# Loading and storing an unpooling kernel's images in three contiguous sections, with reads that span several partitions' rows

## The chip, the cores and the metric

One core of one Trainium2 chip. The metric is the time of one execution in device microseconds (us), lower is better. A ratio is the mean time of one kernel's fast runs over the mean of the other's fast runs of the same rounds on the same chip, so it is not quite the ratio of the medians that are quoted beside it.

## The reference

For each element of `x` (16 x 64 images of 32 x 32, float32) an index from 0 to 3 says in which corner of its 2 x 2 block of the output (64 x 64 an image) it goes. The other three get zero.

```python
for i in range(h):
    for j in range(w):
        idx = indices[b, c, i, j]
        output[b, c, i * 2 + idx // 2, j * 2 + idx % 2] = x[b, c, i, j]
```

The indices arrive as 64-bit integers, of which VectorE reads the low words. So 4.19 MB of x and 8.39 MB of indices are read and 16.78 MB are written: 29.36 MB.

## The kernel before

Each of the 128 partitions holds eight consecutive images. x comes in one load, the indices in two (three images of each partition, then five), all issued by SyncE as its first instructions. VectorE makes one output corner at a time, `(index == corner) * x`. After every two images of a partition, a store of 4 MB is issued on the same SyncE queue. In the trace the transfers land in the order of issue on this queue (x at 12.39 us, the indices at 19.67 and 31.80, the first store at 41.52). Cuts are marked.

```python
G = 2                    # images of a partition in one store
FIRST = 3                # images of a partition in the first index load
x_v = x.rearrange("b (ch t) h w -> (b ch) (t h w)", t=T)            # T = 8
idx_v = indices.rearrange("b (ch t) h w -> (b ch) (t h w)", t=T).bitcast(I32)
out_v = out.rearrange("b (ch g t) oh ow -> g (b ch) (t oh ow)", g=NG, t=G)
# ... out_t: three buffers, the fourth store uses the first again
program.first(nc.sync.dma_start(out=x_t, in_=x_v).then_inc(x_in, 16))
for half, part in enumerate((slice(0, cut), slice(cut, None))):     # cut = FIRST * 2 * N
    program.first(nc.sync.dma_start(out=idx_t[:, part], in_=idx_v[:, part])
                  .then_inc(idx_in[half], 16))
# ... VectorE waits for x_in and idx_in[0], at image FIRST for idx_in[1]
            for pidx in range(4):
                op = nc.vector.scalar_tensor_tensor(
                    out=o_c[:, k : k + n, :, pidx // 2, :, pidx % 2],
                    in0=idx_c[:, t : t + n], scalar=pidx, in1=x_c[:, t : t + n],
                    op0=mybir.AluOpType.is_equal, op1=mybir.AluOpType.mult)
            if k + n == G:
                op.then_inc(made, 1)
for g in range(NG):
    nc.sync.wait_ge(made, g + 1)
    nc.sync.dma_start(out=out_v[g], in_=out_t[g]).then_inc(stored if g else stored_0, 16)
```

## Time and profile before

| | before |
|---|---|
| time, median (range) of 6 runs | 71.62 us (71.49 to 71.75) |
| span of the profiled execution | 70.5 us |
| DMA engines at work | 97.4% of the span |
| VectorE at work | 50% of the span |
| loads landed / last store landed | 31.80 / 70.46 us |
| first store issued | 28.73 us |

The page's row of 40 slices of the span (busy share of the 16 DMA engines in tenths, then GB/s; a packet is booked whole in a slice, so single slices swing):

```profile
DMA  9779798899988999969899997979798999979790
GB/s 260 316 316 558 335 558 344 376 432 446 595 372 372 395 511 535 418 298 521 372 428 465 409 483 335 539 316 558 335 521 372 446 446 409 483 335 539 316 558 37
```

The second is the windows around the place where the queue passes from loads to stores, near 31 us (columns: stretch, length, VectorE, GpSimd, clock, DMA share, GB/s):

```profile
4.00:20.00 16.00, 0.19 (x1) 0.00 (x0) 1.00 1.01 434
20.00:28.00 8.00, 8.00 (x4) 0.00 (x0) 1.00 1.06 461
28.00:33.00 5.00, 5.00 (x5) 0.00 (x0) 1.00 0.90 390
33.00:40.00 7.00, 7.00 (x7) 0.00 (x0) 1.00 1.04 449
40.00:69.00 29.00, 15.40 (x7) 0.00 (x0) 1.00 1.01 434
```

The time from issue to landing of the two index loads:

```profile
DMA to landing us min/median/max: 19.2/25.1/30.9
```

The later one, issued near 0.9 us, lands near 31.8. The 390 in the middle window is a matter of booking: the neighbours have 461 and 449.

### The profile page before, as it was taken

Reading aid. Unit: us, or ns where it says so; the run is one execution under the profiler, and the core shown is the slowest. Engines: PE = TensorE matmul, PEld = TensorE weight load, DVE = VectorE, ACT = ScalarE, POOL = GpSimd, SP = SyncE. Lnnn points to the kernel's source line nnn. Section 1 sums busy time; section 2 is a strip of 40 time slices with the busy share of each in tenths; the row PEclk is TensorE's granted clock in tenths of the full one; section 3 lists DMA queues with packets and bytes.
Section 4 is the critical chain, followed back from the end, with each engine's and each line's share of the span. In section 5 each row is a group of like instructions: output and inputs, shape, how many; then the busy total and the mean of one; then the engine's idle time right before and its main releaser. Section 6 shows DMA issues by size and latency. Waiting matters only on the chain.

```text
span 70.5 us, 72 instructions
## 1 busy us (share of the span) xinstructions
DVE 35.6 (50%) x20; POOL 0.2 (0%) x4
## 2 busy tenths in 40 slices
DVE  0000000000079999999999999999999400000000
POOL 1000000000000000000000000000000000000000
DMA  9779798899988999969899997979798999979790
GB/s 260 316 316 558 335 558 344 376 432 446 595 372 372 395 511 535 418 298 521 372 428 465 409 483 335 539 316 558 335 521 372 446 446 409 483 335 539 316 558 37
DMA packets 1008, 29.36 MB, mean 416 GB/s; under 512 B 112, under 2 KB 112, under 8 KB 112
## 3 DMA queue, kind: packets, MB, share of 16 engines
q1 hardware_dynamic: 1008, 29.36, 97.4%
HBM read 12.58 MB, written 16.78 MB: 416 GB/s over the span
## 4 chain that ended last, share of the span: by engine, by line
DVE 46%; DVEq 4%; issue 1%
DVE out_t L130 46%; DVEq L180 4%
## 5 line engine op out<-in xcount | busy, mean ns | idle before, releaser
L130 DVE SCALAR_TENSOR_TENSOR out_t<-idx_t,x_t 128x2048 f32<-128x2048 int32 (+1 forms) x20 | 35.6, 1857 | 19.8 <-DVEq L119 19.8
L166 POOL MEMSET const-uint8-127<- 128x1 uint8 x1 | 0.1, 103 | 0.0
L166 POOL MEMSET const-bfloat16-1.0<- 128x1 bf16 x1 | 0.1, 102 | 0.0
L166 POOL MEMSET const-float32-0.0<- 128x1 f32 x1 | 0.1, 99 | 0.2 <-issue 0.2
L166 POOL MEMSET const-float32-1.0<- 128x1 f32 x1 | 0.1, 99 | 0.0
## 6 DMA issues: line engine op xcount, KB each, us to landing
out_dram<-out_t SPq DMA_DIRECT2D x4, 4096.0 KB, 13.8
idx_t<-in_indices_dram SPq DMA_DIRECT2D x1, 5120.0 KB, 30.9
x_t<-in_x_dram SPq DMA_DIRECT2D x1, 4096.0 KB, 12.4
idx_t<-in_indices_dram SPq DMA_DIRECT2D x1, 3072.0 KB, 19.2
```

What stands on the lines that cost most here:

```text
L130: op = nc.vector.scalar_tensor_tensor(out=o_c[:, k : k + n, :, pidx // 2, :, pidx % 2], in0=idx_c[:, t : t + n], scalar=pidx, in1=x_c[:, t ...
L166: nc = _bacc.Bacc("TRN2", target_bir_lowering=False, num_devices=1)
L180: with _tile.TileContext(nc) as tc:
```

## The change

The images are cut in three sections of 2, 3 and 3 images for each partition, and each section is one contiguous piece of x, of the indices and of the output in HBM. x and indices are loaded section by section, so VectorE can begin after 3 MB instead of 7. In every load but the first, one read spans the rows of two or four partitions (a widened read, below). The stores are three, of 32, 48 and 48 KB rows, and the last uses the space of inputs already read, so no store has to land before a buffer is used again. The intent is larger pieces, fewer stores, an earlier start of VectorE and no reuse wait. The diff, cut to its core:

```diff
-    def first(self, made):
+    def first(self, made, rows_per_read=1):
         moved = ins.pop()
+        if rows_per_read > 1:
+            (src,) = moved.ins
+            (step, rows), (one, n) = src.ap
+            n *= rows_per_read
+            wide = copy.replace(src, ap=[[n, rows // rows_per_read], [1, n]])
+            moved = copy.replace(moved, ins=[wide], ant_dge_precooked=False)
 # ...
-    G = 2
-    FIRST = 3
-    x_v = x.rearrange("b (ch t) h w -> (b ch) (t h w)", t=T)
+    SECTIONS = (2, 3, 3)
+    X_ROWS = (1, 4, 4)
+    IDX_ROWS = (2, 2, 2)
+    x_i = x.rearrange("b ch h w -> (b ch) (h w)")
 # ...
+        for s, n in enumerate(SECTIONS):
+            imgs = slice(img, img + n * P)
+            for tile_, hbm, rows in ((x_t[s], x_i, X_ROWS[s]), (idx_t[s], idx_i, IDX_ROWS[s])):
+                program.first(
+                    nc.sync.dma_start(
+                        out=tile_, in_=hbm[imgs].rearrange("(p t) n -> p (t n)", t=n)
+                    ).then_inc(arrived[s], 16), rows_per_read=rows)
 # ...
-            if g == NG - 1:
-                nc.vector.wait_ge(stored_0, 16).then_inc(stored_0, -16)
+            nc.vector.wait_ge(arrived[s], 32).then_inc(arrived[s], -32)
 # ...
-        for g in range(NG):
-            nc.sync.wait_ge(made, g + 1)
-            nc.sync.dma_start(out=out_v[g], in_=out_t[g]).then_inc(
+        for s in range(NS):
+            nc.sync.wait_ge(made, s + 1)
+            nc.sync.dma_start(out=out_v[s], in_=out_t[s]).then_inc(stored, 16)
```

More of the change, by code (lines that the diff above doesn't have):

```diff
@@ L1 @@
+import copy
 from contextlib import ExitStack
@@ L20, in __init__ @@
         self.kernel_block = nc.cur_bb.bb.name
-        self.moved = 0
     def __enter__(self):
@@ L37, in first @@
         moved = ins.pop()
-        at = next(k for k, i in enumerate(ins) if i.engine == moved.engine)
-        ins.insert(at + self.moved, moved)
-        self.moved += 1
+        if rows_per_read > 1:
+            (src,) = moved.ins
+            (step, rows), (one, n) = src.ap
+            assert step == n and one == 1 and rows % (16 * rows_per_read) == 0
+            assert 4 * n * rows_per_read <= bass.MAX_DMA_LAST_DIM
+            n *= rows_per_read
+            wide = copy.replace(src, ap=[[n, rows // rows_per_read], [1, n]])
+            moved = copy.replace(moved, ins=[wide], ant_dge_precooked=False)
+        at = next(
+            k
+            for k, i in enumerate(ins)
+            if i.engine == moved.engine and isinstance(i, mybir.InstDrain)
+        )
+        ins.insert(at, moved)
     def last(self, made):
@@ L73 @@
     n_img = B * C
-    T = n_img // P
-    assert T * P == n_img and C % T == 0
-    G = 2
-    NG = T // G
-    FIRST = 3
-    N = H * W
-    x_v = x.rearrange("b (ch t) h w -> (b ch) (t h w)", t=T)
-    idx_v = indices.rearrange("b (ch t) h w -> (b ch) (t h w)", t=T).bitcast(I32)
-    out_v = out.rearrange("b (ch g t) oh ow -> g (b ch) (t oh ow)", g=NG, t=G)
-    x_t = nc.alloc_sbuf_tensor("x_t", [P, T * N], F32).ap()
-    idx_t = nc.alloc_sbuf_tensor("idx_t", [P, T * 2 * N], I32).ap()
+    N = H * W
@@ L87 @@
+    SECTIONS = (2, 3, 3)
+    X_ROWS = (1, 4, 4)
+    IDX_ROWS = (2, 2, 2)
+    assert sum(SECTIONS) * P == n_img
+    NS = len(SECTIONS)
+    x_i = x.rearrange("b ch h w -> (b ch) (h w)")
+    idx_i = indices.rearrange("b ch h w -> (b ch) (h w)").bitcast(I32)
+    out_i = out.rearrange("b ch oh ow -> (b ch) (oh ow)")
+    inputs = nc.alloc_sbuf_tensor("inputs", [P, sum(SECTIONS) * 3 * N], F32).ap()
     out_t = [
-        nc.alloc_sbuf_tensor(f"out_t{g}", [P, G * 4 * N], F32).ap()
-        for g in range(NG - 1)
-    ]
@@ L91 @@
-    out_t.append(out_t[0])
-    x_in = nc.alloc_semaphore("x_in")
-    idx_in = [nc.alloc_semaphore(f"idx_in{g}") for g in range(2)]
+        nc.alloc_sbuf_tensor(f"out_t{s}", [P, n * 4 * N], F32).ap()
+        for s, n in enumerate(SECTIONS[:-1])
+    ]
+    assert SECTIONS[-1] * 4 <= sum(SECTIONS[:-1]) * 3
+    out_t.append(inputs[:, : SECTIONS[-1] * 4 * N])
+    arrived = [nc.alloc_semaphore(f"arrived{s}") for s in range(NS)]
     made = nc.alloc_semaphore("made")
-    stored_0 = nc.alloc_semaphore("stored_0")
@@ L97 @@
     stored = nc.alloc_semaphore("stored")
-    x_c = x_t.rearrange("p (t i j) -> p t i j", t=T, j=W)
-    idx_c = idx_t.rearrange("p (t i j two) -> p t i j two", t=T, j=W, two=2)[
-        :, :, :, :, 0
-    ]
-    cut = FIRST * 2 * N
-    with Program(nc) as program:
-        program.first(nc.sync.dma_start(out=x_t, in_=x_v).then_inc(x_in, 16))
-        for half, part in enumerate((slice(0, cut), slice(cut, None))):
-            program.first(
-                nc.sync.dma_start(out=idx_t[:, part], in_=idx_v[:, part]).then_inc(
-                    idx_in[half], 16
-                )
-            )
-        nc.vector.wait_ge(x_in, 16).then_inc(x_in, -16)
-        for t in range(T):
-            g, k = t // G, t % G
-            if t in (0, FIRST):
-                half = int(t == FIRST)
-                nc.vector.wait_ge(idx_in[half], 16).then_inc(idx_in[half], -16)
-            if k == 1 and t != FIRST:
-                continue
-            n = 1 if k == 1 or t + 1 == FIRST else 2
-            if g == NG - 1:
-                nc.vector.wait_ge(stored_0, 16).then_inc(stored_0, -16)
-            o_c = out_t[g].rearrange(
-                "p (m i two j wo) -> p m i two j wo", m=G, two=2, wo=2, j=W
@@ new lines @@
+    x_t, idx_t, out_v = [], [], []
+    with Program(nc) as program:
+        img, col = 0, 0
+        for s, n in enumerate(SECTIONS):
+            imgs = slice(img, img + n * P)
+            x_t.append(inputs[:, col : col + n * N])
+            idx_t.append(inputs[:, col + n * N : col + 3 * n * N].bitcast(I32))
+            for tile_, hbm, rows in (
+                (x_t[s], x_i, X_ROWS[s]),
+                (idx_t[s], idx_i, IDX_ROWS[s]),
+            ):
+                program.first(
+                    nc.sync.dma_start(
+                        out=tile_, in_=hbm[imgs].rearrange("(p t) n -> p (t n)", t=n)
+                    ).then_inc(arrived[s], 16),
+                    rows_per_read=rows,
+                )
+            out_v.append(out_i[imgs].rearrange("(p t) n -> p (t n)", t=n))
+            img += n * P
+            col += n * 3 * N
+        for s, n in enumerate(SECTIONS):
+            nc.vector.wait_ge(arrived[s], 32).then_inc(arrived[s], -32)
+            if s == NS - 1:
+                nc.vector.wait_ge(made, s)
+            x_c = x_t[s].rearrange("p (i j) -> p i j", j=W)
+            idx_c = idx_t[s].rearrange("p (i j two) -> p i j two", j=W, two=2)[
+                :, :, :, 0
+            ]
+            o_c = out_t[s].rearrange(
+                "p (i two j wo) -> p i two j wo", two=2, wo=2, j=W
@@ L130 @@
                 op = nc.vector.scalar_tensor_tensor(
-                    out=o_c[:, k : k + n, :, pidx // 2, :, pidx % 2],
-                    in0=idx_c[:, t : t + n],
+                    out=o_c[:, :, pidx // 2, :, pidx % 2],
+                    in0=idx_c,
                     scalar=pidx,
-                    in1=x_c[:, t : t + n],
+                    in1=x_c,
                     op0=mybir.AluOpType.is_equal,
@@ L137 @@
                 )
-            if k + n == G:
-                op.then_inc(made, 1)
-        for g in range(NG):
-            nc.sync.wait_ge(made, g + 1)
-            nc.sync.dma_start(out=out_v[g], in_=out_t[g]).then_inc(
-                stored if g else stored_0, 16
-            )
-        nc.sync.sem_inc(made, -NG)
-        program.last(
-            nc.sync.wait_ge(stored, 16 * (NG - 1)).then_inc(stored, -16 * (NG - 1))
-        )
+            op.then_inc(made, 1)
+        for s in range(NS):
+            nc.sync.wait_ge(made, s + 1)
+            nc.sync.dma_start(out=out_v[s], in_=out_t[s]).then_inc(stored, 16)
+        nc.sync.sem_inc(made, -NS)
+        program.last(nc.sync.wait_ge(stored, 16 * NS).then_inc(stored, -16 * NS))
 _INS = ['x', 'indices', 'kernel_size']
```

## The prediction

> **What bounds the kernel now.** I read the page first, then the windows, then the instructions in order of time, then the shapes of the VectorE work, and last the packet records of the trace. The page:
>
> ```profile
> span 70.5 us, 72 instructions
> DVE 35.6 (50%) x20; POOL 0.2 (0%) x4
> ...
> q1 hardware_dynamic: 1008, 29.36, 97.4%
> HBM read 12.58 MB, written 16.78 MB: 416 GB/s over the span
> ...
> DVE 46%; DVEq 4%; issue 1%
> ```
>
> VectorE works half the span; the DMA engines work 97.4% of it. The last line is the chain of waits, which runs through VectorE because that is what issues a store. It accounts for 51% of the span only and stops at the last VectorE instruction (55.4 us); the queue's backlog, which really sets the end, is in no chain. So the question is whether the DMA engines ever run dry or slow. The windows (stretch in us, its length, VectorE, GpSimd, clock, DMA share, GB/s):
>
> ```profile
> 0.00:1.00 1.00, 0.00 (x0) 0.20 (x4) 1.00 0.00 0
> 1.00:2.50 1.50, 0.00 (x0) 0.00 (x0) 1.00 1.24 350
> 2.50:4.00 1.50, 0.00 (x0) 0.00 (x0) 1.00 0.81 350
> 4.00:12.00 8.00, 0.00 (x0) 0.00 (x0) 1.00 1.02 439
> ...
> 20.00:30.00 10.00, 10.00 (x6) 0.00 (x0) 1.00 1.06 459
> 30.00:40.00 10.00, 10.00 (x9) 0.00 (x0) 1.00 0.97 419
> 40.00:50.00 10.00, 10.00 (x5) 0.00 (x0) 1.00 0.97 419
> 50.00:60.00 10.00, 5.40 (x3) 0.00 (x0) 1.00 1.03 442
> 60.00:69.40 9.40, 0.00 (x0) 0.00 (x0) 1.00 0.98 422
> 69.40:70.50 1.10, 0.00 (x0) 0.00 (x0) 1.00 0.01 0
> ```
>
> Nothing moves in the first us and nothing in the last; 1.0 to 4.0 runs at 350 GB/s; all the rest is near 430 (a packet is booked whole in one window, hence 419 beside 459 and shares over 1). No dip separates loads from stores.
>
> The packet records say it exactly. They sort into 16 back-to-back rows, one for each DMA engine, and no row has a gap over 3 ns between its first packet and its last. A packet is one row of one partition: 24 KB takes 912 ns, 32 KB 1213, 40 KB 1514, the 4-byte semaphore write 9. The slope is (1514 - 912) / 16384 B, so 27.2 B per ns; the rest is 8.5 to 9 ns a packet, of which some 3.5 ns overlap the next record (218 ns over the 63 packets of a row), so about 5 ns count. The first packet of 14 rows starts at 1.01 to 1.41 us and takes 1.5 to 2.2 us instead of 1.21; the 15th row starts at 1.81, the 16th at 2.35. That 16th row ends last, at 70.12, its semaphore lands at 70.46, and the span ends. So the span is 2.35 (start of the latest engine) + 67.77 (its uninterrupted packets) + 0.38 (landing and end) = 70.50 us. The time of 71.57 holds 1.07 us more outside the span.
>
> **What the Trainium skill says.** "DMA: Bandwidth & Descriptors", section "Where 436 GB/s comes from": 16 ports of 32 B at 850 MHz make 435.2 GB/s. The trace agrees: 27.2 B per ns and engine is that pace. So 29.36 MB need at least 67.46 us, and 67.77 is within 0.31 us of it. Same page, "Why small descriptors are slow (HBM only)": a fixed 3 cycles or so for each packet, 3.5 ns at 850 MHz; the trace has about 5 (0.31 us over 63 packets). "SBUF — State Buffer", section "SBUF: two separate sides": engines and DMA cannot contend. It agrees: packets take 1213 ns with VectorE at work and without. "Perfetto Trace Analysis", section "DMA Optimizations": splitting transfers helps when the DMA engines are generally idle. Here they are not, and that is what caps this change.
>
> **The change, part by part.** Bytes and issuing queue stay as they are.
>
> *Earlier first work.* The first VectorE instruction waits now for x whole and the first 3 MB of the indices. The instructions in time, and the VectorE work by shape:
>
> ```profile
> 0.43 0.90 SPq L109 DMA_DIRECT2D idx_t<-in_indices_dram  x2
> ...
> 19.81 35.59 DVE L130 SCALAR_TENSOR_TENSOR out_t<-idx_t,x_t 128x2048 f32<-128x2048 int32 x20 [19.81 <-DVEq L119]
> 28.73 27.03 SPq L143 DMA_DIRECT2D out_dram<-out_t  x4
> ```
>
> ```profile
> L130 DVE SCALAR_TENSOR_TENSOR out_t<-idx_t,x_t 128x2048 f32<-128x2048 int32 x12 | 26.6, 2284 | 19.8 <-DVEq L119 19.8
> L130 DVE SCALAR_TENSOR_TENSOR out_t<-idx_t,x_t 128x1024 f32<-128x1024 int32 x8 | 9.2, 1217 | 0.0
> ```
>
> The slope is (2284 - 1217) / 1024 = 1.042 ns an element, so a 3072-element instruction takes 2284 + 1067 = 3351 ns. Afterwards: section 0 is 8 rows of 8 KB (309.5 ns each) and 8 of 16 KB (611 ns) on each engine, 7.4 us; x, of 9.7 us, landed at 12.4, so add 2.7: it lands near 10.1 instead of 19.7. Sections 1 and 2 have 8 x (460 + 912) = 11.0 us each: 21.0 and 32.0. VectorE works 10.1 to 19.2 (4 x 2.284), 21.0 to 34.5 (4 x 3.351) and 34.5 to 47.9; its sum, 35.9, hardly moves. Stores are issued at about 19.2, 34.5 and 47.9. When are they needed? The queue is still loading until about 31; then the first store fills it to 41 (8 rows x 1213 ns), the second to about 55.5 (8 rows of 48 KB at 1816), the third to 70. So the three are 12, 6 and 8 us early. Before, the first store was issued at 28.73, 2.4 us before the loads had all landed (31.1 for the first of the 16 engines), and the last at 55.4, some 4 us early. They were early too, and no engine ran dry. The margin grows; the time gains nothing.
>
> *No reuse wait.* The last store no longer needs the first one's buffer. That wait cost nothing before: VectorE's 35.59 us of work fill the 35.59 us from 19.81 to 55.40 without a gap, so the first store had landed before VectorE came to its buffer: 0 us.
>
> *Packets.* Before, each engine runs 24 load and 32 store rows and 7 semaphore writes: 63. After: 24 store rows and 9 semaphore writes, and loads of 48 pieces if the writes count (one for each partition) or 24 if the wider reads do (8+4+2+4+2+4). So 81 or 57 packets; at 5 ns, +0.09 or -0.03 us. The contiguous sections cannot raise the rate, since strided rows already go at 27.2 B per ns.
>
> *Issue.* Six load issues instead of three; three took 1.33 us (0.38, then 0.90 for two), so six take about 2.7. The first carries 2.5 us of data, so the second, out before 1 us, is not missed. The widened reads are made by another path of the build (they lose a mark of being prepared in advance) and may take longer to issue; up to 2 us each is hidden.
>
> *Start.* The only real room. Engines ended between 69.44 and 70.12, mean 69.69, and their lags come wholly from the first packet. With 8 KB first rows, close together in HBM, the stagger may change. If the slowest came down to the mean, that is 0.43 us; if all became like the best, 0.68. Nothing in the profile says which way it goes. I take 0.25 us off as an estimate.
>
> Sum: -0.25 (start) + 0.03 (packets) + 0 + 0 = -0.2, so 71.35 us.
>
> **The rivals.** (1) The start improves on every engine: all begin at 1.01 us with no stretched first packet. Then 70.12 becomes 1.01 + 67.77 = 68.78, and the time 70.2 (1.9% less). For it: first rows a quarter the size. Against: the first packets were stretched by 0.3 to 0.95 us beyond their bytes, which looks like a latency that a smaller row pays as well. (2) A hole in the queue: the issue of a widened read is slow, or its two sides, cut differently, stall an engine at row borders. One hole of 1 us makes 72.4; 10% lower pace in the five widened loads (11.5 MB, 26.5 us) would make 74. For it: no such read in the trace of before. Against: three loads of different shapes ran at one pace with no gap at their seams. (3) Stores with VectorE idle were slowed by distance between rows: then contiguous rows would gain. Against: stores and loads both run 1213 ns for 32 KB, at 128 KB and at 32 KB pitch.
>
> **Range and chances.** Steady part: -0.03 to +0.09. Start: -0.7 to +0.3, and three runs before spread 0.18. That gives 70.75 to 71.85 for 8 in 10. Over 2% faster needs 1.43 us, more than rival 1 in full: 2%. Over 2% slower needs rival 2: 4%. Within 2%: 94%.
>
> **What would show it.** In the profile after: DMA share 97% or more, and about 430 GB/s in every window from 4 us to the end (right), or a dip beside a seam or in the loads (rival 2); the first VectorE instruction near 10 us and the last ended near 48, with the span shrinking by under 0.7 us all the same; the windows between 1 and 4 us above 350 GB/s if the start gained. The prediction is wrong if the span falls below 69.2, or if a stretch between 4 and 69 us is under 400 GB/s.

## The result and the profile after

The median is 72.92 us (72.75 to 73.00, 6 runs) against 71.62 before: ratio 1.0179, 95% interval 1.0160 to 1.0198. The predicted range ended at 71.85. The change costs 1.3 us. From the page of the changed kernel:

```profile
span 71.7 us, 65 instructions
...
DMA  3999899899999999939999999999999999999990
GB/s 55 393 466 549 347 439 439 384 439 439 439 439 439 439 439 439 439 146 457 421 457 421 466 412 439 439 439 439 439 439 439 439 439 439 439 439 439 439 439 0
DMA packets 912, 29.36 MB, mean 410 GB/s; under 512 B 144, under 2 KB 144, under 8 KB 144
...
q1 hardware_dynamic: 912, 29.36, 97.0%
```

The busy share is as high as before, 97.0%, yet fewer GB/s come out of it. One slice stands out, the 18th (30.5 to 32.3 us), with 3 tenths and 146 GB/s. Seen this way it looks like a pause. The windows (columns as before) show that it is a slow stretch in which packets that started earlier are still running:

```profile
4.00:20.00 16.00, 8.90 (x4) 0.00 (x0) 1.00 1.02 440
20.00:28.00 8.00, 7.11 (x3) 0.00 (x0) 1.00 1.11 473
28.00:33.00 5.00, 5.00 (x2) 0.00 (x0) 1.00 0.90 301
33.00:40.00 7.00, 6.97 (x3) 0.00 (x0) 1.00 0.99 426
40.00:69.00 29.00, 7.25 (x3) 0.00 (x0) 1.00 1.01 437
```

From 28 to 33 us the share is 0.90, as before, but 301 GB/s come out in place of 390: the engines are occupied and move less. The other windows differ from those of before by 3 to 23 GB/s, in both directions, which is a matter of booking: in the packet records these packets are at or within 33 ns of their regular time. The instructions in order of time (start, length, engine, line, operation) show what is queued there:

```profile
2.95 0.59 SPq L128 DMA_DIRECT2D inputs<-in_indices_dram  x1
9.89 8.90 DVE L149 SCALAR_TENSOR_TENSOR out_t<-inputs 128x2048 f32<-128x2048 int32 x4 [9.89 <-DVEq L138]
18.82 15.60 SPq L161 DMA_DIRECT2D out_dram<-out_t  x2
20.89 13.17 DVE L149 SCALAR_TENSOR_TENSOR out_t<-inputs 128x3072 f32<-128x3072 int32 x4 [2.10 <-DVEq L138]
34.09 13.17 DVE L149 SCALAR_TENSOR_TENSOR inputs<-inputs 128x3072 f32<-128x3072 int32 x4
47.28 0.33 SPq L161 DMA_DIRECT2D out_dram<-inputs  x1
```

VectorE starts at 9.89 us and ends near 47.3, and the first store is issued at 18.82, each within 0.7 us of the prediction. The landing of the index loads:

```profile
DMA to landing us min/median/max: 9.3/19.1/29.9
```

The last of them was issued at 2.95, so it landed near 32.9 us; the prediction had 32.0 and the kernel before 31.8. By the landings in the trace, the loads end 1.10 us later than before (32.90 against 31.80) and the stores take 38.74 us in place of 38.67. That is the 1.17 us by which the span grew.

The packet records put it in one place. Each engine's last load packet, 48 KB that begin at 28.99 to 29.47 us, takes 2.32 to 3.23 us; the load packets of 48 KB before it take 1.815 to 1.848. The mean over the 16 engines is 1.0 us too much, and the latest engines have 1.3 to 1.4. From the next packet on, a store row, everything is at its regular time again. So the question is what slows the last 48 KB of loading.

### The profile page after: what moved, and what is told of

Its sections match the earlier page's. It is cut to its first block, busy times and chain, and to the rows that moved or that the text cites. A ratio compares the mean times of both kernels' runs of the same rounds, so it can differ in the third digit from the quotient of the medians.

```text
span 71.7 us, 65 instructions
## 1 busy us (share of the span) xinstructions
DVE 35.2 (49%) x12; POOL 0.2 (0%) x4
## 5 line engine op out<-in xcount | busy, mean ns | idle before, releaser
L149 DVE SCALAR_TENSOR_TENSOR out_t<-inputs 128x2048 f32<-128x2048 int32 (+1 forms) x8 | 22.1, 2821 | 12.0 <-DVEq L138 12.0
L149 DVE SCALAR_TENSOR_TENSOR inputs<-inputs 128x3072 f32<-128x3072 int32 x4 | 13.2, 3354 | 0.0
```

Of the source, the lines that this page charges most:

```text
L149: op = nc.vector.scalar_tensor_tensor(out=o_c[:, :, pidx // 2, :, pidx % 2], in0=idx_c, scalar=pidx, in1=x_c, op0=mybir.AluOpType.is_equal ...
```

## The experiments

The seam is the place where the queue passes from loads to stores. "Stretch" below is the time by which load packets that start between 26 and 33 us exceed the regular time of their size (bytes at 27.2 B per ns and 8.5 ns), in the mean of the 16 engines. The loads' landing is that of the last engine's semaphore write. The table comes from the packet records and the results of the runs:

| run | first store issued, us | stretch, us | loads landed, us | time (median), us | ratio to before |
|---|---|---|---|---|---|
| before | 28.73 | 0.00 | 31.80 | 71.62 | 1 |
| after | 18.82 | 1.03 | 32.90 | 72.92 | 1.0179 |
| e1_rows1 | 18.86 | 1.02 | 32.93 | 73.11 | 1.0188 |
| e2_last_plain | 18.76 | 1.28 | 33.13 | 73.15 | 1.0191 |
| e3_only_last | 18.86 | 1.33 | 33.21 | 73.16 | 1.0179 |
| e5_strided | 18.89 | 1.06 | 32.71 | 72.75 | 1.0141 |
| e6_swap_last | 18.79 | 1.10 | 32.86 | 73.02 | 1.0186 |
| e7_exchanged | 18.77 | 1.05 | 32.79 | 72.94 | 1.0174 |
| e10_before_early | 26.15 | 1.13 | 32.61 | 73.62 | 1.0270 |
| e4_late_store | 27.50 | 1.01 | 32.80 | 73.05 | 1.0178 |
| e12_store_at_28 | 27.85 | 0.72 | 32.70 | 72.77 | 1.0139 |
| e13_rows1_at_29 | 28.60 | 0.13 | 31.67 | 71.77 | 1.0010 |
| e9_store_at_29 | 28.80 | 0.05 | 31.87 | 71.73 | 1.0013 |
| e11_store_at_31 | 30.76 | 0.03 | 31.69 | 72.36 | 1.0093 |
| e8_held_store | 34.01 | 0.03 | 31.67 | 75.65 | 1.0552 |

All gave correct results. Of the edits below the core is shown; lines that only keep the semaphore counts right are left out.

### First round: the widened reads, or the early store

Theory W blamed the new kind of read, theory Q the store that stands in the queue for 12 us.

**e1_rows1** takes the widening from every load.

```diff
-    X_ROWS = (1, 4, 4)
-    IDX_ROWS = (2, 2, 2)
+    X_ROWS = (1, 1, 1)
+    IDX_ROWS = (1, 1, 1)
```

> All six loads read one partition's row at a time again; sections, buffers, contiguous stores and early issue stay. Theory W (the widened reads make the 1.0 us stretch of every engine's last load packet and the small stretches before it): no stretch at the load-to-store seam, each packet within 10 ns of its size's time, span 70.1 to 70.7, time 71.3 to 71.8, ratio to before 0.995 to 1.005. Theory Q (the first store stands in the queue 12 us before its turn, and that makes the stretch): seam still 0.5 to 1.4 us, time 72.7 to 73.1.

73.11 us: the stretch is all there. It now lies on the last two packets of each engine, of 24 KB each (0.40 to 0.69 us too long on the last, up to 0.79 on the one before), so on the last 48 KB again. Theory W falls. The small stretches of up to 33 ns that the widened packets had before that place are gone (at most 8 ns are left). By their place in the queue the 26 to 32 ns belong to the x packets of section 2; the widened index packets have up to 14.

**e2_last_plain** takes it from the last load only (`IDX_ROWS = (2, 2, 1)`), **e3_only_last** leaves it on the last load only (`X_ROWS = (1, 1, 1)`, `IDX_ROWS = (1, 1, 2)`).

> Only the last index load reads one row at a time; the four loads before it stay widened. Theory W in its narrow form (the widened load that stands right before the first store pays): seam stretch gone, the stretches of 26 to 32 ns stay, time 71.6 to 72.0. Theory W in its wide form (a lag gathered over all widened loads comes out at the first place it must be made good): some 1 us of stretch stays, now somewhere in the last load, time 72.6 to 72.9. Theory Q: 72.7 to 73.1.

> Only the last index load is widened, two rows a read; all others read one row at a time. Narrow W: seam stretch of 0.5 to 1.4 us is there, time 72.5 to 73.0. Wide W (gathered over five loads): stretch a third or less, time 71.6 to 72.1. Theory Q: 72.7 to 73.1.

73.15 and 73.16 us, with 1.28 and 1.33 us of stretch: neither form of W explains that. Together with e1 this says that the stretch does not need the widening. In e3 it reaches further back: on seven engines the 48 KB packet before the last is slow too (1.96 to 2.17 us).

**e4_late_store** issues the first store when VectorE is half through section 1.

```diff
+                if s == 1 and pidx == 1:
+                    op.then_inc(made, 1)
             op.then_inc(made, 1)
-                nc.vector.wait_ge(made, s)
+                nc.vector.wait_ge(made, s + 1)
-            nc.sync.wait_ge(made, s + 1)
+            nc.sync.wait_ge(made, s + 2)
```

> Loads widened as in the change; the first store is held back until VectorE is half through section 1 (near 27.5 us instead of 18.8), still 3 us before the loads end. Theory Q: seam stretch gone, time 71.5 to 72.0. Theory W: the stretch stays at 0.5 to 1.4 us, time 72.7 to 73.1.

73.05 us, stretch 1.01: by its expectation Q falls too. Later runs showed that Q was right in kind and the hold was 1 us too short.

### Second round: place, layout, or the turn from loads to stores

Four theories: P (the close rows of a contiguous section), L (the place in HBM), R (the tail of the loads, whatever stands behind it) and T (the turn from loads to stores that stand ready).

**e5_strided** keeps sections, order and sizes, but gives each partition its eight consecutive images back, so nothing is contiguous across partitions.

```diff
-    x_i = x.rearrange("b ch h w -> (b ch) (h w)")
+    x_i = x.rearrange("b (ch t) h w -> (b ch) t (h w)", t=8)
-            imgs = slice(img, img + n * P)
+            imgs = slice(img, img + n)
-                        out=tile_, in_=hbm[imgs].rearrange("(p t) n -> p (t n)", t=n)
+                        out=tile_, in_=hbm[:, imgs].rearrange("p t n -> p (t n)")
```

(The indices and the output likewise, and no widened reads.)

> Sections, issue order, sizes and buffers as in the change, but every partition keeps its eight consecutive images as before: loads and stores of a section are strided in HBM (x rows at 32 KB pitch, indices at 64 KB, outputs at 128 KB), no widened reads. Theory P (the contiguous section, its close rows, slows the last 48 KB of reading on each engine): stretch near 30 us gone, time 71.3 to 71.8. Theories T (turn from loads to stores that have stood ready) and R (the tail of the last load, whatever it reads): stretch of about 1 us stays, time 72.7 to 73.2.

72.75 us, stretch 1.06: the contiguous layout is not the cause. The time is a little better than e1's, which has the same reads and sections. I leave that small difference open.

**e6_swap_last** loads the indices of section 2 before its x; **e7_exchanged** exchanges the places of sections 1 and 2 in HBM.

```diff
-            )
+            )[:: -1 if s == NS - 1 else 1]:          # e6
-            imgs = slice(img, img + n * P)
+            first = (0, 5, 2)[s] * P                 # e7
+            imgs = slice(first, first + n * P)
```

> In section 2 the indices are loaded before x; all else as in the change. Theory L (the place in HBM, the end of the indices): the stretch moves to about 24 to 28 us and the last x load is clean. Theories T and R: the stretch stays on the last load before the stores, now an x row near 29 us, 0.5 to 1.4 us on each engine. Time 72.7 to 73.1 in both.

> Sections 1 and 2 exchange their places in HBM (images 640 to 1023 are loaded and stored second, 256 to 639 last). Theory L: the stretch moves to the end of section 1's loads, near 18 to 20 us. Theories T and R: it stays near 29 us. Time 72.7 to 73.1 in both.

In both the stretch stays near 29 us on whatever load is last (an x packet in e6). The place in HBM is not it.

**e8_held_store** holds the first store back until the loads have long landed.

```diff
-            nc.sync.wait_ge(made, s + 1)
+            nc.sync.wait_ge(made, max(s + 1, 2))
```

> The first store is held back until section 1 is made as well (34 us), some 3 us after the last load has landed, so the queue runs dry in between. Theory T: the last load's packets take 1815 to 1850 ns, no stretch, last landing near 31.7 us. Theory R: stretch of 0.5 to 1.4 us all the same, last landing near 32.9. Time some 2 to 3 us longer than the change's, 75 to 76, in both.

The stretch is gone. The landing of the index loads in this run, and its windows:

```profile
DMA to landing us min/median/max: 9.3/19.0/28.6
```

```profile
28.00:33.00 5.00, 5.00 (x2) 0.00 (x0) 1.00 0.37 157
33.00:40.00 7.00, 6.96 (x3) 0.00 (x0) 1.00 0.88 374
```

28.6 in place of 29.9 from issue to landing: the loads land at 31.67. All 16 last packets take 1829 ns. The price here is a queue that stands empty (share 0.37), hence 75.65 us. The run tells two things. The loads alone do not slow at their end, so the store behind them is needed for it (theory T). And the first store packet starts at 34.86, so 0.85 us pass from an issue to its first packet. e4's store, issued at 27.50, was therefore ready at 28.35, still ahead of the last 48 KB of loads, which begin at 28.9 to 29.4. The store of the kernel before was ready only at 28.73 + 0.85 = 29.58. That made theory T2: the loads are slowed if the store is ready when their last 48 KB or so begin.

### Third round: the same kernel with a later store, the kernel before with an earlier one

**e9_store_at_29** splits one VectorE instruction of section 1 (a third, then two thirds) and issues the first store after the first of the two parts. Nothing else is changed.

```diff
+                pieces = (slice(0, n * H),)
+                if s == 1 and pidx == 2:
+                    pieces = (slice(0, H), slice(H, n * H))
+                for k, part in enumerate(pieces):
                     op = nc.vector.scalar_tensor_tensor(
-                    out=o_c[:, :, pidx // 2, :, pidx % 2],
+                        out=o_c[:, part, pidx // 2, :, pidx % 2],
+                    if len(pieces) == 2 and k == 0:
+                        op.then_inc(made, 1)
```

> The change as it is, but the first store is issued near 28.8 us (on a third of VectorE's third instruction of section 1), as late as in the kernel before (28.73). Theory T2 (the last reads of the loads are slowed only when the store already stands in the queue as they begin; about 1 us passes from issue to first packet, so the border is an issue near 28 us): the last load packet takes 1815 to 1850 ns instead of 2.3 to 3.2 us, last landing of the loads near 31.7, no hole, span 70.2 to 70.6, time 71.4 to 71.8, ratio to before 0.994 to 1.004. Rival (any store issued before the loads have landed does it, and the kernel before was spared by its layout or its load shapes): stretch of 0.5 to 1.4 us stays, time 72.7 to 73.1.

71.73 us in 6 runs, ratio 1.0013 (0.9992 to 1.0034). The landing, the windows and the instructions in order of time:

```profile
DMA to landing us min/median/max: 9.4/19.2/28.9
```

```profile
20.00:28.00 8.00, 6.99 (x3) 0.00 (x0) 1.00 1.13 485
28.00:33.00 5.00, 5.00 (x3) 0.00 (x0) 1.00 0.86 367
33.00:40.00 7.00, 6.97 (x3) 0.00 (x0) 1.00 1.04 449
```

```profile
28.80 5.81 SPq L167 DMA_DIRECT2D out_dram<-out_t  x2
```

One issue time moved by 10 us takes the whole loss away. The last packets take 1856 ns in the mean (2120 on one engine), and the queue never runs empty: the first store packets start at 30.98 to 31.48, right behind.

**e10_before_early** is the opposite: the kernel before with one constant changed.

```diff
-    FIRST = 3
+    FIRST = 2
```

> The kernel before with one constant changed (FIRST 2 instead of 3): the first index load is 2 MB, VectorE starts near 17.4 us and the first store is issued near 26.5 us instead of 28.73. Nothing else of the change is in it. Theory T2: the last load packets of every engine are stretched by about 1 us in all, last landing of the loads near 32.8 instead of 31.8, time 72.5 to 73.0, ratio 1.012 to 1.02. Rival (layout, load shapes or sections are needed for it): no stretch, time 71.4 to 71.9.

73.62 us, more than either theory expected. From its instructions in order of time, its windows, and the landing of its index loads:

```profile
17.23 8.90 DVE L130 SCALAR_TENSOR_TENSOR out_t<-idx_t,x_t 128x2048 f32<-128x2048 int32 x4 [17.23 <-DVEq L119]
26.15 33.47 SPq L143 DMA_DIRECT2D out_dram<-out_t  x4
32.75 26.51 DVE L130 SCALAR_TENSOR_TENSOR out_t<-idx_t,x_t 128x2048 f32<-128x2048 int32 x12 [6.63 <-DVEq L119]
```

```profile
28.00:33.00 5.00, 0.25 (x1) 0.00 (x0) 1.00 0.85 269
```

```profile
DMA to landing us min/median/max: 16.7/24.2/31.7
```

With the first store out at 26.15 every engine's last load packet (48 KB here) takes 2.72 to 3.20 us, a stretch of 1.13, and the loads land at 32.61. Nothing of the change is in this kernel: no contiguous piece, no widened read, no section. What I had overlooked is the rest of the time: VectorE must now wait until 32.75 for the second index load, so the second store comes late, and each engine is empty for 0.5 to 1.2 us near 42 us. The span grew by 0.81 us through the landing and by some 0.98 through that hole. Its 28 to 33 us window also has the idle VectorE beside the stretch, which shows that VectorE's work is not what slows the packets.

**e11_store_at_31** issues the store on the third instruction of section 1 as a whole (`if s == 1 and pidx == 2` in e4's edit).

> The change with the first store issued on the third instruction of section 1, near 30.9 us, so that its first packets can run from about 31.9, just after the loads' last (31.3 to 31.7 when not stretched). T2: no stretch, a hole of 0.3 to 0.8 us on each engine in its place, time 71.8 to 72.3. Rival as above: stretch stays, 72.7 or more.

72.36 us, just above the range: no stretch, and each engine stands empty for 0.42 to 0.82 us before the first store packet (the earliest comes 0.84 us after the issue, as in e8). So an issue near 28.8 us, 3 us before the loads land, is close to the optimum from both sides: 1 us earlier costs the stretch, 2 us later costs a hole.

### Fourth round: the border, and the widened reads at a clean seam

**e12_store_at_28** is e9 with the first piece a quarter as large, so that the store is issued at 27.85; **e13_rows1_at_29** is e9 with the widening taken out as in e1.

> The first store issued near 27.9 us, between the run where the stretch stood (27.50) and the run where it was gone (28.80). The last 48 KB of loads on each engine begin at 28.9 to 29.4, and an issue takes about 1 us to its first packet, so 28.9. T2 (what counts is whether the store is there as the last reads begin): the engines that begin their last load piece latest are stretched, the earliest not or little; stretch of 0.2 to 0.9 us in the mean of the engines, but since the latest engine ends the span the time is 72.2 to 72.9. Rival (the border is about 2.2 us before the loads' end and sharp, all engines alike): either all engines at 0.5 to 1.4 us and 72.8 to 73.1, or none and 71.5 to 71.9.

> The late store of e9 with all loads read one partition's row at a time: what the widened reads are worth once the seam is clean. By packets (24 more on each engine at some 5 ns) it should be 0.12 us slower than e9; by the stretches of 26 to 100 ns that widened index reads show, 0.1 to 0.2 us faster. Both are small: time 71.5 to 71.9, ratio to before 0.997 to 1.004. With 24 KB rows the last two load packets were both stretched in e1; a late store near 28.8 us should leave both at 912 ns. If instead the first of them is still stretched, it is the last 48 KB that count and not the last packet.

e12: 72.77 us, stretch 0.72. Ready at 27.85 + 0.85 = 28.70, the store was ahead of all 16 last packets (28.85 to 29.44). Two engines were hardly slowed (1.83 and 1.89 us), the others took 2.23 to 2.96. The two mildest began at 28.85 and 29.23, so the order of starts, which the expectation named, does not sort them cleanly. The border lies between 27.85 (14 engines slowed) and 28.80 (e9, two engines slowed, by 0.15 and 0.29 us) and goes engine by engine; what decides for one engine stays open. So T2 holds roughly and not packet by packet, and since the loads end at about the same time in all these runs, they do not separate a border in bytes (48 KB) from one in time (a store issued some 3 us before the loads land).

e13: 71.77 us, ratio 1.0010 (0.9986 to 1.0035), the same as e9's 1.0013. At a clean seam the widened reads are worth nothing that these runs can tell. In e13 the second-last packets are clean and seven engines have 0.17 to 0.36 us on the last one: issued 0.2 us before e9's, this store is on the border.

## Why the prediction was wrong

**The step that failed** is the part *Earlier first work*. Its times came out: section 0 landed at 9.76 us (10.1 predicted without the gain at the start), VectorE's three stretches ended at 18.8, 34.1 and 47.3 (19.2, 34.5, 47.9), and the stores were issued as early as computed. The conclusion, "The margin grows; the time gains nothing", took an early store to be free. It costs 1.1 us, by which the loads land later: the margin itself is the fault. The prediction had all numbers to see that the change moved the first store's issue from 28.73 to about 19 us, and no reason in the profile of before to see a cost in it, since there the store was issued 3 us before the loads landed and nothing was slowed. e9 (store moved back, 71.73) and e10 (store moved forward in the old kernel, stretch 1.13) show the cost in both directions.

**Slips in its working**, none of which makes the 1.1 us. The 2.4 us from the first store's issue to the loads' landing is to the first engine's landing (31.1); the last is at 31.80, 3.1 us after. The 1.07 us outside the span pairs the time of one execution with the span of another: the profiled one took 71.82 us, so 1.3 lie outside. VectorE's stretches are 8.90, 13.17 and 13.17 us where it multiplied means to 9.1, 13.4 and 13.4: neighbouring instructions overlap a little, as its own line shows (12 x 2284 ns make 27.4, and 26.6 are busy). The terms of its range add up to 70.84 to 71.96 before the spread of the runs, so its upper end of 71.85 was too low; the measured 72.92 lies outside either way.

**The rivals.** Rival 2 had the direction, slower by a fault in the queue, and named the marker, a dip beside a seam. Its cause, widened reads with sides cut differently or slow to issue, is refuted by e1, e2 and e3. A widened load takes 0.53 to 0.61 us to issue against 0.38 to 0.73 for a plain one in e13, and hides. Rival 1 did not come: eight engines start at 1.00 to 1.08 us, the other eight only at 1.80 to 2.03. Nor did rival 3: contiguous store rows of 32 KB take the same 1213 ns.

**The start** came out at -0.25 us in the profiled run: section 0 landed 2.44 us after what its packets add up to, x before 2.69 after. In e9 it was -0.14 by the same reckoning. The sign that the prediction named, over 350 GB/s from 1 to 4 us, did not appear (322 GB/s in the changed kernel). The gain shows nowhere in the time of e9, because of the next point.

**Packets.** The records count the reads: 912 in all, 57 an engine, the variant with -0.03. The term missed that widened packets run over, those of x in section 2 by 27 and 33 ns, index packets by up to 14, some 0.14 us an engine in all. By the landings sections 1 and 2 of e9 take 10.99 to 11.01 us each where 6 x 1.815 makes 10.89, so +0.2 us in all. That eats the start. Without widening the packets are more (81 an engine) and the sum is the same (e13).

**No reuse wait** was right at 0: the wait had cost nothing, and its removal gained nothing (e9 is level with before). So was the argument that the rate cannot rise: from 33 us on both kernels move their store rows at the regular time, 38.74 against 38.67 us in all.

**The chances** had 94% on "within 2%", which held by a hair (1.0179) and by luck: the 1.1 us that decide were in no term. The range did not hold: for slower I had allowed only +0.3 us outside rival 2.

## What to carry to other kernels

When one queue carries first all loads and then the stores, look at when the first store is issued, not only whether it is in time. Here a store ready before the last 48 KB an engine of the loads begin cost 1.1 us, one issued about 3 us before the loads land cost nothing, and one 2 us later left a hole. So a split that only lets the first store come sooner can lose, and here, with the DMA engines 97% busy, what was lost lay at the seam: read the packets' lengths there, because the busy share does not show a packet that is merely slow. No version tried beats the kernel before: e9 and e13 are level with it. Whether a store on another queue than that of the loads costs the same was not tried.

## What the Trainium skill lacked or had wrong

- No page has it: with a store standing in SyncE's queue behind the loads, the last 48 KB of loads on an engine take 2.32 to 3.23 us (the changed kernel) instead of the 1.83 that all engines have when the store is held to 34.01 us (e8), and 14 of 16 when it is issued at 28.80 (e9). It belongs to "DMA: Bandwidth & Descriptors", section "Queues, rings and completion order". What in the DMA engine does it, no run shows.
- "DMA: Bandwidth & Descriptors", section "Rules for kernel authors", says to issue a DMA early so that its fixed cost overlaps, and names no exception. For the first store behind loads on one queue it was wrong here: issued at 18.82 us the kernel took 72.92 us, issued at 28.80 us 71.73 us.
- Same page, "Why small descriptors are slow (HBM only)": about 3 cycles a packet, 3.5 ns by an estimate at the 850 MHz that the page gives for the fabric; the 63 packets of an engine here carried about 5 ns each above the bytes' time.
- No page gives the pace of loads whose reads span several partitions' rows: packets of 48 KB took 1815 ns for x of section 1, 1842 and 1848 for x of section 2, and 1815 to 1829 for the indices (store rows of 48 KB take about 1815), with no gain in time (e13 against e9, 1.0010 and 1.0013).
